# A two-layer trunk on one core: FFN up-projections by seven block products in place of eight, and the FFN split into two passes

## The chip, the core and the metric

The kernel runs on one core of one Trainium2 chip. The metric is device time in microseconds (us), the median of three runs. TensorE (PE) does the matrix products, VectorE (DVE) and GpSimd (POOL) elementwise arithmetic, ScalarE (ACT) casts and activations, and SyncE (SP) issues the DMAs, all of them in one queue, in program order.

## The reference

Two layers, sequence length 1024, model width 1024, FFN width 2816. What matters here is the second half of each layer, and the norm that stands after it:

```
x = x + gate1 * (concat(mixers(h1)) @ w_out)       # h1 = modulated RMSNorm of x
h2 = rmsnorm(x, g_ffn) * (1 + scale2) + shift2
x = x + gate2 * ((silu(h2 @ w1) * (h2 @ w3)) @ w2)  # w1, w3: 1024 x 2816; w2: 2816 x 1024
...
out = rmsnorm(x, g_final)                          # after the second layer
```

The scales, shifts and gates of a layer come from six small projections of the conditioning vector c, called the mods here.

## The kernel before, in words

x and its norms are held feature-major: eight tiles (`x[d]`, 128 features by 1024 positions), worked on in two halves of 512 positions. Every fp32 matrix product is made of three matmuls on values split into a high part (a cast on ACT, L152 for weights) and a low part (value minus high part, `sub_lo`, L160, on POOL for weights and on DVE for activations): high by high (L181), low by high (L182) and high by low (L183). A matmul has 128 by 128 weights and 512 columns. So one block of 128 outputs of an up-projection, for one half of the positions, takes 8 x 3 = 24 matmuls.

The FFN (`ffn`) goes over the 22 blocks of 128 hidden units in nine groups of two and one of four. For each group it loads blocks of w1, w3 and w2 (512 KB each, through SP), splits them, makes both up-projections of each block for both halves (`up`), applies silu (L1112), multiplies (L1113), splits the result (L1114, L160), and then adds the group's share of the down-projection to x (`down`, one accumulation of 2 x 3 matmuls per output block and half, added to x by L1121). `side()` puts pieces of the next layer's mods (L269, from 256 KB loads) between groups.

At the beginning of the FFN the norm of the second half (`norm2(1)`) isn't ready: it needs the last piece of the mixers' output projection (L1077), a sum of squares (L354, L355, and L324 on PE), a reciprocal root in twelve tiny DVE instructions (L330 to L146), its broadcast over the partitions (L339, L341 on PE, L343) and then a scaled tile (L383), its high part (L385) and its low part (L390, or L387 and L160 on POOL) for each of eight tiles. The first group makes its down-projection for the first half early, in this place: 48 matmuls that don't need that norm. At the end, the last group has four blocks, so its down-projection of the second half has 96 matmuls, and `between()`, the next norm of the first half (the next layer's, or the final one with its output stores, L1463 and L1465), is run beside them.

The instructions of each engine stand in an order that a scheduler wrote; each engine takes its own strictly in that order.

## Time and profile before

| | |
|---|---|
| median of three runs | 2955.49 us (2949.87 to 2956.98) |
| profiled execution, span from first to last instruction | 2950.3 us |
| PE busy | 2752.1 us, 93% |
| DVE, ACT, POOL busy | 57%, 38%, 27% |
| mean granted TensorE clock | 0.958 of full speed |
| FFN of layer 0, of layer 1 (about) | 808 to 1520 us, 2227 to 2928 us |

The span is that of one profiled execution; no time outside it is listed for this execution, so its span is compared with the runs' times as it stands. Matmuls are pipelined: a row's duration (0.39 us at full clock) overlaps the next one's, and the pitch from start to start is what counts.

### The profile page before, as it was taken

What the parts mean: (1) busy time and instruction counts of PE and PEld (TensorE: products, weight loads), DVE (VectorE), ACT (ScalarE), POOL (GpSimd) and SP (SyncE); (2) the same over time, 40 slices, a digit from 0 to 9 for tenths busy, and PEclk for the clock granted to TensorE, in tenths of its full rate; (3) what the DMA queues carried; (4) which work ended last, traced back from release to release, by engine and by line L of the source; (5) the groups of instructions that cost most, each with busy time, mean ns of one, the idle gap of its engine ahead of it and who ended that gap; (6) DMA issues with size and microseconds to landing.
All of it is one profiled execution on the core that took longest, in us unless ns stands there. A gap on an engine that the chain in (4) does not pass through costs nothing.

```text
span 2950.3 us, 34304 instructions
## 1 busy us (share of the span) xinstructions
PE 2752.1 (93%) x12818; PEld 2224.0 (75%) x12832; DVE 1667.1 (57%) x3456; ACT 1129.8 (38%) x2204; POOL 788.3 (27%) x412
## 2 busy tenths in 40 slices
PE   4897988999799999999999889999989999999997
PEld 4775856778678888888878667787867888888886
DVE  7579877765764444333165897787474222333215
ACT  4454777854321111111235557775342111111111
POOL 4232134441432112223231420032133222211220
PEclk9898979999999999999999988999999999999998
DMA  6102233232143222311111022112211111111101
GB/s 245 53 19 83 63 130 93 76 136 78 48 145 113 93 86 86 106 51 58 58 64 54 33 76 81 43 32 87 82 58 44 50 43 57 51 43 43 50 29 57
DMA packets 71847, 213.57 MB, mean 72 GB/s; under 512 B 9089, under 2 KB 9985, under 8 KB 71681
## 3 DMA queue, kind: packets, MB, share of 16 engines
q1 hardware_dynamic: 71680, 211.39, 21.3%
q8 instruction: 100, 1.64, 0.2%
q14 instruction: 67, 0.54, 0.1%
HBM read 184.29 MB, written 19.73 MB: 69 GB/s over the span
## 4 chain that ended last, share of the span: by engine, by line
PE 60%; DVE 8%; ACT 2%; issue 1%; POOL 0%; DMA 0%; DVEq 0%; ACTq 0%; POOLq 0%
PE tr L183 8%; PE tr L181 8%; PE tr L182 8%; PE s L181 6%; PE s L183 6%; PE s L182 6%; PE mm L181 4%; PE mm L183 4%; PE mm L182 4%; DVE jv L531 2%; PE tr L666 1%; ACT ja L528 1%; PE tr L694 1%; DVE t L383 1%; PE pv L687 1%
## 5 line engine op out<-in xcount | busy, mean ns | idle before, releaser
L160 POOL TENSOR_TENSOR wl<-raw,wh 128x1024 fp32r<-128x1024 f32 (+1 forms) x190 | 453.2, 2388 | 1262.9 <-ACT wh L152 1189.3
L152 ACT ACTIVATE wh<-raw 128x1024 fp32r<-128x1024 f32 (+2 forms) x170 | 175.1, 1033 | 752.9 <-PE mm L182 355.5
L1113 DVE TENSOR_TENSOR t<-t,tr 128x512 f32<-128x512 f32 x84 | 57.7, 687 | 581.5 <-PE tr L183 574.8
L183 PE MATMUL tr<-h,wl 128*128 128x512 f32 x928 | 368.9, 398 | 0.0
L181 PE MATMUL tr<-h,wh 128*128 128x512 f32 x928 | 368.3, 397 | 0.1
L182 PE MATMUL tr<-h,wh 128*128 128x512 f32 x928 | 367.1, 396 | 0.0
L182 PE MATMUL s<-h,wh 128*128 128x512 f32 x704 | 279.4, 398 | 5.7 <-DVE h L390 5.6
L181 PE MATMUL s<-h,wh 128*128 128x512 f32 x704 | 280.0, 398 | 5.0 <-ACT h L385 5.0
L183 PE MATMUL s<-h,wl 128*128 128x512 f32 x704 | 278.4, 395 | 0.0
L181 PEld LDWEIGHTS tr<-h,wh 128*128 128x128 f32 x928 | 175.8, 189 | 42.7 <-issue 1.2
L183 PEld LDWEIGHTS tr<-h,wl 128*128 128x128 f32 x928 | 175.5, 189 | 41.8 <-issue 1.0
L1121 DVE SCALAR_TENSOR_TENSOR x<-mm,modc,x 128x512 f32<-128x512 f32 x160 | 119.7, 748 | 153.9 <-PE mm L183 153.9
L182 PEld LDWEIGHTS tr<-h,wh 128*128 128x128 f32 x928 | 175.6, 189 | 40.4
L528 ACT ACTIVATE ja<-score,tk_t 128x384 bf16<-128x384 f32 (+2 forms) x160 | 146.0, 912 | 120.0 <-DVE tk_t L550 86.6
L642 ACT ACTIVATE P<-P,mx 128x128 f32<-128x128 f32 (+1 forms) x192 | 142.9, 745 | 62.3 <-DVE mx L639 46.7
L182 PEld LDWEIGHTS s<-h,wh 128*128 128x128 f32 x704 | 133.6, 190 | 39.0 <-DVE h L390 7.6
L181 PEld LDWEIGHTS s<-h,wh 128*128 128x128 f32 x704 | 133.5, 190 | 36.4 <-ACT h L385 5.4
L669 ACT ACTIVATE Th<-tr 128x512 fp32r<-128x512 f32 (+3 forms) x288 | 128.3, 469 | 81.2 <-PE tr L666 74.0
L183 PEld LDWEIGHTS s<-h,wl 128*128 128x128 f32 x704 | 133.3, 189 | 31.1
L160 DVE TENSOR_TENSOR Tl<-tr,Th 128x512 fp32r<-128x512 f32 (+2 forms) x232 | 131.4, 587 | 39.4 <-ACT Th L669 38.7
L666 PE MATMUL tr<-ident,P 128*128 128x128 f32 x816 | 142.1, 289 | 2.6 <-DVE y L699 1.1
L160 DVE TENSOR_TENSOR al<-t,ah 128x512 fp32r<-128x512 f32 x84 | 109.2, 1304 | 59.0 <-ACT ah L1114 46.0
(357 smaller groups left out, 6347.1 us busy)
## 6 DMA issues: line engine op xcount, KB each, us to landing
raw<-w SPq DMA_DIRECT2D x88, 512.0 KB, 3.3
mraw<-w_mod SPq DMA_DIRECT2D x48, 512.0 KB, 6.3
t<-w_mod SPq DMA_DIRECT2D x96, 256.0 KB, 4.5
raw<-ffn_w SPq DMA_DIRECT2D x44, 512.0 KB, 3.3
raw<-w_fm SPq DMA_DIRECT2D x30, 512.0 KB, 3.5
raw<-wo_abd SPq DMA_DIRECT2D x16, 384.0 KB, 3.1
x<-xT SPq DMA_DIRECT2D x16, 256.0 KB, 6.1
raw<-w_tm SPq DMA_DIRECT2D x8, 512.0 KB, 3.3
```

The lines of the kernel that those rows point to most:

```text
L152: self.nc.scalar.activation(out, in_, AF.Copy)
L160: (eng or self.nc.vector).tensor_tensor(out=out, in0=in_, in1=hi.bitcast(F32), op=ALU.subtract)
L181: self.nc.tensor.matmul(out, lh, rh, start=(i == 0), stop=False)
L182: self.nc.tensor.matmul(out, lh, rl, start=False, stop=False)
L183: self.nc.tensor.matmul(out, ll, rh, start=False, stop=(stop and i == n - 1))
L528: nc.scalar.activation(ja, score[t], AF.Sign, bias=c, scale=-1.0, accum_out=o)
L531: v.tensor_scalar(out=jv, in0=up[t] if step < 16 else score[t], scalar1=c, scalar2=0.0, op0=ALU.is_ge, op1=ALU.subtract, accum_out=o)
L642: nc.scalar.activation(P[:, 0:nk], P[:, 0:nk], AF.Exp, bias=m[:, j:j + 1], scale=-1.0, accum_out=st["rs"][:, i:i + 1])
L666: nc.tensor.transpose(p[:, i * 128:(i + 1) * 128], P[:, (kts[n] - k0) * 128:(kts[n] - k0 + 1) * 128], self.ident)
L669: nc.scalar.activation(Th[:, cs].bitcast(F32) if len(js) <= few else Th[:, cs], p[:, cs], AF.Copy)
L1113: nc.vector.tensor_tensor(out=s, in0=s, in1=p3, op=ALU.mult)
L1121: nc.vector.scalar_tensor_tensor(out=x[d][:, hs], in0=p, scalar=self.modc[l][:, 40 + d:41 + d], in1=x[d][:, hs], op0=ALU.mult, op1=ALU.add)
```

## The change

The first two blocks of the FFN are projected as before, but their down-projection isn't made early. The other 20 blocks are taken in ten pairs. Such a pair, for both halves of the positions and both halves of the width, is a 2 x 2 by 2 x 2 block product, and is made of seven block products of 4 x 3 = 12 matmuls in place of eight (Strassen's form). The sums of weight blocks that this needs (s1 to s4 of each of w1 and w3) are made on DVE for every pair, and all seven are split (cast on ACT, low part on POOL). The combinations of h2 (`combos`, t1 to t4) are made once per layer from the unsplit t tiles, which norm2 now keeps. The products' results are combined on DVE.

The hidden activations aren't split then but stored in DRAM (`aspill`), as is x (`x2spill`). In a second pass, for each half of the positions, all eight output blocks are accumulated in eight PSUM banks over all 22 blocks; w2 is loaded and split once for each half, each activation tile is loaded back and split. In the second half the first four blocks (LATE) use seven banks, then `between()` runs with the eighth bank, and then the 12 matmuls held back for that bank follow.

```diff
-            if gi == 0:
...
-                if early:
-                    side()
-                    for d in range(KD):
-                        down(d, HALVES[0])
...
+    def up_pair(self, l, fa, H, T, side):
...
+        B11, B21, B22 = H[0][0:4], H[0][4:8], H[1][4:8]
...
+        def seven(name, o, X, Y, Z):
...
+            with self.tc.high_priority(offset=PRIO):
+                W[1] = self.split_tile(a11, nc.gpsimd)
+                v.tensor_tensor(out=s1, in0=a21, in1=a22, op=ALU.add)
+                v.tensor_tensor(out=s2, in0=s1, in1=a11, op=ALU.subtract)
+                W[6] = self.split_tile(s2, nc.gpsimd)
+                W[5] = self.split_tile(s1, nc.gpsimd)
+                v.tensor_tensor(out=s3, in0=a11, in1=a21, op=ALU.subtract)
+                W[7] = self.split_tile(s3, nc.gpsimd)
+                W[2] = self.split_tile(a12, nc.gpsimd)
+                v.tensor_tensor(out=s4, in0=a12, in1=s2, op=ALU.subtract)
+                W[3] = self.split_tile(s4, nc.gpsimd)
+                W[4] = self.split_tile(a22, nc.gpsimd)
+            p1, p6, p5, p7 = [self.bank(o + i) for i in range(4)]
+            product(p1, W[1], B11, True)
+            nc.scalar.activation(X, p1, AF.Copy)
+            product(p6, W[6], T[2], True)
+            v.tensor_tensor(out=X, in0=X, in1=p6, op=ALU.add)
+            product(p5, W[5], T[1], True)
+            v.tensor_tensor(out=Y, in0=X, in1=p5, op=ALU.add)
+            product(p7, W[7], T[3], True)
+            v.tensor_tensor(out=Y, in0=Y, in1=p7, op=ALU.add)
+            product(p1, W[2], B21, False)
+            product(p5, W[3], B22, False)
+            v.tensor_tensor(out=Z, in0=X, in1=p5, op=ALU.add)
+            product(p7, W[4], T[4], False)
+            v.tensor_tensor(out=X, in0=X, in1=p7, op=ALU.add)
+            return p1
...
+        p = seven("w1", 0, X, Y, Z)
+        nc.scalar.activation(V, p, AF.Silu)
+        for t in (Y, Z, X):
+            nc.scalar.activation(t, t, AF.Silu)
+        side()
...
+        p = seven("w3", 4, X3, Y3, Z3)
+        v.tensor_tensor(out=V, in0=V, in1=p, op=ALU.mult)
...
+        for g, hs in enumerate(HALVES):
+            for d in range(KD):
+                nc.sync.dma_start(out=x[d][:, hs], in_=self.x2spill[l][d][:, hs])
+            late = LATE if g else 0
+            banks = [self.bank(d) for d in range(KD - 1 if late else KD)]
+            for f in range(NF):
+                w, y = load(f), act(f, g)
+                for d in range(len(banks)):
+                    step(banks[d], w, y, f, d)
+                if f < late:
+                    held.append((w, y))
+                if f == late - 1:
+                    between()
+                    banks.append(self.bank(KD - 1))
+                    for i, (w, y) in enumerate(held):
+                        step(banks[KD - 1], w, y, i, KD - 1)
+            for d in range(KD):
+                nc.vector.scalar_tensor_tensor(out=x[d][:, hs], in0=banks[d], scalar=self.modc[l][:, 40 + d:41 + d],
```

The first place to look at is PE's order where norm2(1) of layer 1 is made. Before, the four ones-matmuls of the sum of squares (L324) are followed by early down matmuls (their weights are `ah` and `al`), 15 of them until the first broadcast (L341), 21 more until the first matmul on the new norm:

```order
L183 MATMUL tr_19301<-ah_18963,wl_18954 128x512
L324 MATMUL pv_19176<-ones,t_19153 128x1 x4
L181 MATMUL tr_19269<-ah_19032,wh_18959 128x512
L181 MATMUL tr_19285<-ah_19032,wh_18959 128x512
L181 MATMUL tr_19301<-ah_19032,wh_18959 128x512
L182 MATMUL tr_19269<-al_19033,wh_18959 128x512
L183 MATMUL tr_19269<-ah_19032,wl_18960 128x512
```

In the changed kernel the same place reads as follows (`mh`, `ml` are the mixers' output, `h_19554` the first tile of the new norm):

```order
L181 MATMUL mm_19481<-mh_19279,wl_18669 128x512
L324 MATMUL pv_19512<-ones,t_19489 128x1 x4
L341 MATMUL mm_19538<-t_19539,ones 128x128
L341 MATMUL mm_19538<-t_19542,ones 128x128
L341 MATMUL mm_19538<-t_19545,ones 128x128
L341 MATMUL mm_19538<-t_19548,ones 128x128
L179 MATMUL s_19687<-h_19554,wh_19297 128x512
L179 MATMUL tr_19712<-h_19554,wh_19303 128x512
L179 MATMUL s_19740<-h_19554,wh_19362 128x512
L179 MATMUL tr_19765<-h_19554,wh_19368 128x512
L180 MATMUL s_19687<-h_19554,wh_19297 128x512
```

The early down matmuls are gone from between the steps of the norm, and nothing has taken their place; layer 0 reads the same.

The second place is DVE's order in a pair of layer 1, from the end of its w1 products to the sums for its w3 products (`raw_20192`, `raw_20193` are this pair's w3, `raw_20325`, `raw_20326` the next pair's w1; L1153 makes s1, L1157 s3, L1154 s2 and L1160 s4):

```order
L1171 TENSOR_TENSOR act_20059<-act_20059,tr_20094 128x512
L1174 TENSOR_TENSOR act_20058<-act_20059,tr_20093 128x512
L1176 TENSOR_TENSOR act_20059<-act_20059,tr_20094 128x512
L1153 TENSOR_TENSOR su_20196<-raw_20193 128x512
L1157 TENSOR_TENSOR su_20197<-raw_20192,raw_20193 128x512
L1153 TENSOR_TENSOR su_20329<-raw_20326 128x512
L1154 TENSOR_TENSOR su_20196<-su_20196,raw_20192 128x512
L1154 TENSOR_TENSOR su_20329<-su_20329,raw_20325 128x512
L1160 TENSOR_TENSOR su_20197<-raw_20192,su_20196 128x512
L1157 TENSOR_TENSOR su_20330<-raw_20325,raw_20326 128x512
L1160 TENSOR_TENSOR su_20330<-raw_20325,su_20329 128x512
L1167 TENSOR_TENSOR t_20189<-t_20189,s_20224 128x512
```

All sums of w3 stand behind the last addition of the w1 products (L1176), and one sum of the next pair (`su_20329`) stands ahead of s2; all sums for the next pair's w1 are made here too, a whole set of products before they are needed.

The third place is PE's order at the end of layer 1, round the final norm of the first half. Before, down matmuls stand behind L324 (33 of them until L341):

```order
L181 MATMUL mm_23351<-ah_22763,wh_22623 128x512
L182 MATMUL mm_23351<-al_22764,wh_22623 128x512
L183 MATMUL mm_23351<-ah_22763,wl_22624 128x512
L324 MATMUL pv_23258<-ones,t_23235 128x1 x4
L181 MATMUL mm_23351<-ah_22887,wh_22629 128x512
L182 MATMUL mm_23351<-al_22888,wh_22629 128x512
L183 MATMUL mm_23351<-ah_22887,wl_22630 128x512
```

In the changed kernel (`ws_23268` to `ws_23364` are the split activations of the four blocks held back, `ws_23497` the next block's):

```order
L1239 MATMUL tr_23259<-ws_23364,wl_23359 128x512
L324 MATMUL pv_23411<-ones,t_23388 128x1 x4
L341 MATMUL pv_23437<-t_23438,ones 128x128
L341 MATMUL pv_23437<-t_23441,ones 128x128
L341 MATMUL pv_23437<-t_23444,ones 128x128
L341 MATMUL pv_23437<-t_23447,ones 128x128
L1239 MATMUL pv_23476<-ws_23268,wh_23262 128x512 x2
L1239 MATMUL pv_23476<-ws_23268,wl_23263 128x512
L1239 MATMUL pv_23476<-ws_23300,wh_23294 128x512 x2
```

The 84 matmuls of the four blocks now all stand ahead of L324, and between L324 and L341 there is nothing. What comes behind the held matmuls is the block of `ws_23497`, whose load stands in SP's order behind the eight stores of the output:

```order
L1578 DMA out<-t_23467 128x512
L162 DMA raw_23874<-ffn_w 128x1024
L1578 DMA out<-t_23470 128x512
L1578 DMA out<-t_23473 128x512
L1228 DMA t_23495<-aspill_255 128x512
```

In layer 0, where the norm is the next layer's, no output is stored, but ACT's order has the norm's broadcast (L343) and eight casts (L387) and three casts of w2 ahead of the next block's activations (`ws_11865`); its last rows there are:

```order
L387 ACTIVATE h_11833<-t_11834,modc_87 128x512
L387 ACTIVATE h_11838<-t_11839,modc_87 128x512
L149 ACTIVATE wh_11859<-raw_11857 128x1024
L149 ACTIVATE wh_11894<-raw_11892 128x1024
L1093 ACTIVATE ws_11865<-t_11863 128x512
```

In before the down matmuls beside these norms used weights and activations that were split ahead of them.

## Rows read from the trace of the kernel before

**Rows 1.** The page: busy time of each engine.

```profile
PE 2752.1 (93%) x12818; PEld 2224.0 (75%) x12832; DVE 1667.1 (57%) x3456; ACT 1129.8 (38%) x2204; POOL 788.3 (27%) x412
```

**Rows 2.** Windows: PE, PEld, DVE, ACT, POOL busy us (instructions), clock, DMA share, GB/s.

```profile
1000.00:1500.00 500.00, 500.00 (x2172) 407.77 (x2171) 185.99 (x291) 86.50 (x114) 112.83 (x46) 1.00 0.23 76
1500.00:1600.00 100.00, 93.60 (x507) 80.68 (x506) 59.39 (x93) 43.85 (x78) 33.11 (x21) 0.95 0.19 65
2300.00:2900.00 600.00, 600.00 (x2602) 489.24 (x2601) 174.87 (x212) 99.48 (x131) 125.98 (x53) 1.00 0.13 44
```

**Rows 3.** Groups of instructions by line and form: busy us, mean ns, idle before.

```profile
L160 POOL TENSOR_TENSOR wl<-raw,wh 128x1024 fp32r<-128x1024 f32 x172 | 420.6, 2448 | 1152.6 <-ACT wh L152 1083.5 <-DVE t L339 31.2 <-DMA qspill<-saq 16.1
...
L160 POOL TENSOR_TENSOR wl<-raw,wh 128x512 fp32r<-128x512 f32 x2 | 2.6, 1280 | 6.3 <-ACT wh L152 6.3
...
L152 ACT ACTIVATE wh<-raw 128x1024 fp32r<-128x1024 f32 x152 | 160.3, 1058 | 719.3 <-PE mm L182 355.5 <-issue 151.7 <-PE s L182 115.6
...
L1121 DVE SCALAR_TENSOR_TENSOR x<-mm,modc,x 128x512 f32<-128x512 f32 x160 | 119.7, 748 | 153.9 <-PE mm L183 153.9
...
L1113 DVE TENSOR_TENSOR t<-t,tr 128x512 f32<-128x512 f32 x84 | 57.7, 687 | 581.5 <-PE tr L183 574.8 <-ACT t L1112 6.7
...
L1114 ACT ACTIVATE ah<-t 128x512 fp32r<-128x512 f32 x84 | 52.6, 631 | 211.3 <-DVE t L1113 210.6 <-PE tr L183 0.5
```

**Rows 4.** Timeline of PE round norm2(1), layer 1: start, us, engine, instruction, [idle before].

```profile
2213.90 0.50 PE L181 MATMUL tr<-ah,wh 128*128 128x512 f32 x1 [0.78 <-DVE s L1113]
...
2214.70 0.95 PE L324 MATMUL pv<-ones,t 128*128 128x1 f32 x8
...
2220.86 0.49 PE L341 MATMUL mm<-t,ones 128*128 128x128 f32 x2 [1.43 <-DVE t L339]
...
2221.42 0.39 PE L182 MATMUL mm<-al,wh 128*128 128x512 f32 x1
...
2228.20 0.50 PE L181 MATMUL mm<-ah,wh 128*128 128x512 f32 x1 [0.66 <-DVE x L1121]
```

**Rows 5.** Timeline of PE round norm2(0), layer 1.

```profile
2167.15 0.66 PE L181 MATMUL s<-h,wh 128*128 128x512 f32 x1 [2.67 <-ACT h L385]
...
2172.16 0.79 PE L182 MATMUL s<-h,wh 128*128 128x512 f32 x1 [3.93 <-DVE h L390]
2172.76 0.63 PE L183 MATMUL s<-h,wl 128*128 128x512 f32 x1
...
2177.74 0.39 PE L181 MATMUL s<-h,wh 128*128 128x512 f32 x1
```

**Rows 6.** Timeline of PE at the last norm, from the last down matmul on.

```profile
2928.06 0.39 PE L183 MATMUL tr<-ah,wl 128*128 128x512 f32 x1
2934.86 1.87 PE L324 MATMUL pv<-ones,t 128*128 128x1 f32 x8 [6.41 <-DVE t L355]
2939.36 2.04 PE L341 MATMUL pv<-t,ones 128*128 128x128 f32 x8 [2.64 <-DVE t L339]
```

**Rows 7.** Timeline of DVE and ACT behind that broadcast.

```profile
2942.08 5.39 DVE L1463 SCALAR_TENSOR_TENSOR t<-x,gcols,t 128x512 f32<-128x512 f32 x8 [2.27 <-ACT t L343]
...
2941.45 0.60 ACT L343 ACTIVATE t<-pv 128x512 f32<-128x512 f32 x1 [9.32 <-PE pv L341]
```

**Rows 8.** Timeline of PE: the final norm of the first half, beside down matmuls.

```profile
2911.46 0.95 PE L324 MATMUL pv<-ones,t 128*128 128x1 f32 x8
...
2920.34 1.05 PE L341 MATMUL pv<-t,ones 128*128 128x128 f32 x8
```

**Rows 9.** Timeline of DVE and of POOL in layer 0's FFN, two instructions that overlap.

```profile
933.75 2.77 DVE L160 TENSOR_TENSOR al<-t,ah 128x512 fp32r<-128x512 f32 x1
...
933.25 2.73 POOL L160 TENSOR_TENSOR wl<-raw,wh 128x1024 fp32r<-128x1024 f32 x1 [3.17 <-ACT wh L152]
```

**Rows 10.** DMA issues: engine, op xcount, KB each, median us from issue to landing.

```profile
t<-w_mod SPq DMA_DIRECT2D x96, 256.0 KB, 4.5
raw<-ffn_w SPq DMA_DIRECT2D x44, 512.0 KB, 3.3
```

More of the change, by code (lines that the diff above doesn't have):

```diff
@@ L386, in norm_chunk @@
         if k % 2:
-            nc.gpsimd.tensor_scalar(out=t, in0=t, scalar1=b[:, k:k + 1], scalar2=1.0, op0=ALU.add, op1=ALU.mult)
+            u = self.tmp() if kept else t
+            nc.gpsimd.tensor_scalar(out=u, in0=t, scalar1=b[:, k:k + 1], scalar2=1.0, op0=ALU.add, op1=ALU.mult)
+            t = u
             self.sub_lo(h[:, 1, :], t, h[:, 0, :], nc.gpsimd)
@@ new lines, in ffn, with up, act, load @@
+    def ffn(self, l, x, H, T, side, between):
+        nc = self.nc
+        ws, ys = [], [None, None]
+        def up(i, g):
+            hs = HALVES[g]
+            if g == 0:
+                ys[i] = self.slab("act")
+            p1 = self.fm_chunk(H, ws[i][0], g, self.ps("s", (128, 512), 2))
+            p3 = self.fm_chunk(H, ws[i][1], g, self.tr())
+            nc.scalar.activation(ys[i][:, hs], p1, AF.Silu)
+            nc.vector.tensor_tensor(out=ys[i][:, hs], in0=ys[i][:, hs], in1=p3, op=ALU.mult)
+        self.wlo = nc.gpsimd
+        for i in range(2):
+            ws.append((self.load_w(self.a["w1"][l, i]), self.load_w(self.a["w3"][l, i])))
+            up(i, 0)
+        yield
+        for i in range(2):
+            up(i, 1)
+            nc.sync.dma_start(out=self.aspill[l][i], in_=ys[i])
+            side()
+        for fa in range(2, NF, 2):
+            self.up_pair(l, fa, H, T, side)
+            side()
+        H.clear()
+        T.clear()
+        x[:] = [self.slab("x") for _ in range(KD)]
+        held = []
+        def act(f, g):
+            t = self.tmp()
+            nc.sync.dma_start(out=t, in_=self.aspill[l][f][:, HALVES[g]])
+            with self.tc.high_priority(offset=PRIO):
+                return self.split_tile(t, nc.vector)
+        def load(f):
+            return self.load_w(self.a["ffn_w2"][l, f * 128:(f + 1) * 128, :], base=True)
+        def step(p, w, y, f, d):
+            wh, wl = [u[:, d * 128:(d + 1) * 128] for u in w]
+            yh, yl = y[:, 0:512], y[:, 512:1024]
+            for i, (u, r) in enumerate(((wh, yh), (wh, yl), (wl, yh))):
+                nc.tensor.matmul(p, u, r, start=(f == 0 and i == 0), stop=(f == NF - 1 and i == 2))
+        for g, hs in enumerate(HALVES):
[16 more added lines that the diff above has]
+                nc.vector.scalar_tensor_tensor(out=x[d][:, hs], in0=banks[d], scalar=self.modc[l][:, 40 + d:41 + d],
+                                               in1=x[d][:, hs], op0=ALU.mult, op1=ALU.add)
+        between()
@@ L1373, in mixer, with norm2 @@
         H2 = []
-        def norm2(g, r, R=None):
-            H2.append(self.norm_half(x, self.acol[l][:, 8:16], self.modc[l][:, 24:32], g, r, self.mm, R))
+        kept = [[], []]
+        HT = {}
+        def norm2(g, r):
+            a, b = self.acol[l][:, 8:16], self.modc[l][:, 24:32]
+            R = self.stat_bcast(r, self.mm)
+            H2.append([None] * KD)
+            for k in range(4):
+                t = self.slab("t", F32, (128, 2, 512))
+                kept[g].append(t)
+                for j in range(2):
+                    H2[g][k + 4 * j] = self.norm_chunk(x, a, b, HALVES[g], R, k + 4 * j, t[:, j, :])
+            for d in range(KD):
+                nc.sync.dma_start(out=self.x2spill[l][d][:, HALVES[g]], in_=x[d][:, HALVES[g]])
+            if g:
+                HT.update(self.combos(*kept, b))
         rr = []
```

145 lines of the change are left out of this document (66 added, 79 removed).

## The prediction

> **What bounds the kernel now.** I read the page first, then the windows, then the groups by line, then the timeline wherever PE was not busy. The page shows PE busy for 93% of the span, DVE for 57%, ACT 38%, POOL 27% [rows 1]. An average says little, so the windows come next: in both FFNs PE is busy for every microsecond, at full granted clock, while DVE works some 30 to 37 us of 100, POOL 21 to 23 and ACT 17 [rows 2]. So in this stage only PE's matmuls set the time, and the pitch is 500 / 2172 = 0.2302 us and 600 / 2602 = 0.2306 us from one start to the next; I use 0.2304. A matmul less is 0.23 us less, as long as PE stays fed. The timeline shows why it is fed so well: at norm2(1) PE runs early down matmuls between the steps of the norm and idles only 0.78, 1.43 and 0.66 us [rows 4]; at the final norm of the first half it goes straight through, 8.9 us from L324 to L341 [rows 8]. Where nothing stands between, as at the last norm, PE waits 6.41 and 2.64 us [rows 6].
>
> **What is removed.** A pair of hidden blocks took 2 x 2 x 2 x 24 = 192 up matmuls and takes 2 x 7 x 12 = 168. Ten pairs, two layers: 20 x 24 = 480 matmuls, 480 x 0.2304 = 110.6 us. The down matmuls keep their number (22 x 8 x 2 x 3 in both forms). Everything else is what is lost of these 110.6 us.
>
> **A: norm2(1) without cover.** The order shows L324, L341 and the first matmuls on the new norm with nothing between, in both layers. So PE waits through the chain. Its parts: from the last projection to L324 about 1.6 us (2214.70, less the 2213.1 at which PE fell idle ahead of 2213.90, with what it did between left out); from L324 to L341 4.50 us undisturbed [rows 6], of which 0.95 is L324 itself: 3.55; then norm2(0), which has no cover already now, shows what follows L341: 2.67 us idle until the first high part, 3.93 until the first low part [rows 5]. Together 11.75, less the 2.87 idle there now [rows 4]: 8.9 us a layer. Behind it comes the clock: after those two idles matmuls took 0.63 us in place of 0.39 until 2177.7 [rows 5]; some 17 of them at 0.43 us a pitch are 17 x 0.2 = 3.4 us. 12.3 a layer, 24.6 for both. `combos` puts 16 combinations and 8 low parts on DVE behind the norm, about 24 x 0.7 = 17 us by L1113's 687 ns [rows 3], against 96 + 12 matmuls, 25 us, of PE work that starts after the norm's first tile and shares that time with its remaining tiles: I add 2 us a layer. **A = +29**, rounded up. Its bounds: 12, if the low part comes at once and the clock holds; 50, if POOL holds DVE up in norm and combinations.
>
> **B: the change from w1 to w3 in a pair.** Let T be the end of the last w1 product. All sums of w3 stand behind its addition (the order of DVE), and one sum of the next pair is ahead of s2. The addition ends at T + 0.2 + 0.75 (an eviction, 748 ns), and four sums of 0.69 take DVE to T + 3.7; I take L1113's 687 ns for a sum [rows 3], since before has none. Its cast, half a tile wide, is 0.63 on ACT and its low part 1.28 on POOL [rows 3]: T + 4.4 and T + 5.7. PE meanwhile has the first product, which needs no sum: 12 x 0.23 = 2.76, and about 0.3 for its own low part: T + 3.06. So it waits 1.3 us for the cast, then does six high-part matmuls as three casts arrive (0.63 each against 0.46), and is past the low part at about T + 6.1: 2.0 us idle in a pair, 40 in all 20. The other direction, w3 to the next w1, costs nothing, since those sums are ready. Single idles of 1.4 us left the clock up: behind 1.43 us the matmuls still show 0.39 [rows 4]. In layer 0 the mods' instructions stand in some of these places too: +2. **B = +42**, with 10 (the casts run ahead) and 90 (4.5 us a pair) as ends.
>
> **C and D: the second pass.** Its beginning needs w2 and activations that are loaded and split while the last products run: +2 (0 to 12). In its steady course a block of one half has 24 matmuls, 5.53 us. Against that stand 512 KB of w2, landing in 3.3 us [rows 10], a cast of 1.06 and a low part of 2.45 us [rows 3], a chain of 6.8 us, of which two buffers make 3.4 us a block; POOL alone needs 2.45, ACT 1.06 + 0.63, DVE one low part. The evictions of L1121, 160 for each of two sets of banks [rows 3], fall from 320 to 32. All hidden under PE: 0 (0 to 10).
>
> **E: the norm beside four blocks.** The 84 matmuls stand ahead of L324, 19.4 us, which more than covers the eight evictions and the sums of squares; but between L324 and L341 nothing is left: 3.55 us idle. Then PE has L341 and 12 held matmuls, 0.8 + 2.8 = 3.6 us. In layer 1 the next activations are loaded behind the eight stores: from L341 to L1463 2.72 us, its eight instructions 5.39 [rows 6, 7], then a 256 KB load (4.5 us as for the mods, 3.3 as for twice the size of weights [rows 10]; I take 4.0) and a cast, 0.63: 12.7 after L341, so 9.1 idle. In layer 0 the broadcast's end (2.1 us after L341 [rows 6, 7]), eight casts paced by DVE at about 1 us, three of w2 at 1.06 and one of 0.63 come to 13.9: 10.3 idle. With 3.4 for the clock each time, as in A: 3.55 + 9.1 + 3.4 = 16, and 17. **E = +33** (20 to 48); now it costs nothing [rows 8].
>
> **G: the end of layer 0.** The next layer's norm of the first half is ready far earlier than now. Of the 6.4 us idle there now [rows 2] I give back 3: **-3**. The last norm's tail is unchanged: eight evictions and the sums as at 2928.06 to 2934.86 [rows 6].
>
> **The sum.** -110.6 + 29 + 42 + 2 + 0 + 33 - 3 = -7.6 us on the span of 2950.3. That span lies 5.2 under the median of the runs and inside their spread, so I apply the difference to the median: 2947.9, rounded 2948.
>
> **A rule weighed.** A low part on DVE took 2.77 us and ended 0.54 us after the POOL instruction that had started ahead of it [rows 9], where an operation of that size beside no such work is 0.69 [rows 3]. So DVE can lose 2 us to one low part on POOL. In B it shouldn't: by the order POOL is free from about T + 0.7 until s2 is done. The Trainium skill, "SBUF — State Buffer", section "SBUF: two separate sides", says that DVE, with two inputs in SBUF, and a GpSimd instruction that reads SBUF lock each other out for a whole instruction. By that rule the two rows are as they should be, and a sum for the next set that starts just ahead of the first low part would push it by an estimated 0.69 us a pair, 14 us in all, which would make the sum +6 in place of -7.6.
>
> **The rivals.** *The waits are hidden.* If ACT and DVE come to the w3 sums early, B is 10, A 12 and E 20: -110.6 + 12 + 10 + 20 - 3 = -72, 2884 us. Against it speaks the strict order. *The clock falls in every pair* (the other side). B's idle of 2.0 us lies between the 1.43 that left the clock up [rows 4] and the 2.67 and 3.93 behind which it was down [rows 5]. If one sum or low part is held up by 0.7 us, a third of what rows 9 show, and the clock's fall costs 3.4 each time: 20 x 4.1 = 82, 3030 us. It decides when a pair loses more than (110.6 - 29 - 2 - 33 + 3) / 20 = 2.5 us in all, its wait and its slow matmuls together. *w2 bounds the down pass.* If the two buffers didn't overlap, a block would take 6.8 us and not 5.53: 1.27 x 88 = +112, 3060 us. The windows would show PE idle all through the second pass; POOL's 2.45 and DMA's 3.3 speak against it.
>
> **How the numbers follow.** My forecast has a chance of 0.50, hidden waits 0.25, the clock in every pair 0.20, w2 0.05. The likeliest case alone is 2925 to 2968. Both signs hold much of the chance, so the range is wide: 2870 takes in nearly all of the hidden case, 3015 the lower third of the clock case and leaves out the rest and w2. About 0.3%, 9 us, is what a measurement of this kernel can tell from no change. Half of the likeliest case and all of the hidden one, less a little, are faster by more: 0.46. Within it: two fifths of the likeliest, 0.20. Slower: the rest of the likeliest and the last two cases, 0.34.
>
> **What would show it.** A: PE idle of some 10 us at norm2(1), 0.63 us matmuls behind it. B: in each pair an idle of about 1.3 us ahead of the second w3 product, by the cast of s2, then some tenths; if that idle is 0 B is wrong, if it is 2.5 or the clock of the windows in the up pass is under 1.00, the rival is right. E: two idles, 3.5 us ahead of L341 and 9 to 10 behind the held matmuls. D: windows of the second pass at PE 100%. The forecast falls if the matmuls themselves keep another pitch than 0.2304.

## The result and the profile after

| | before | after |
|---|---|---|
| median in the same comparison | 2952.68 us | 2979.71 us (2977.92 to 2981.84) |
| ratio | | 1.0095, interval 1.008 to 1.011 |
| profiled execution, span | 2950.3 us | 2977.4 us |
| mean granted TensorE clock | 0.958 | 0.941 |
| moved by DMA | 213.57 MB | 299.64 MB |

The changed kernel is 0.95% slower. The forecast was a gain of 7.6 us; the two spans show a loss of 27.1. The time lies inside the range, on the other side of no change, and 35 us are to be found.

The page of after, busy time of each engine, answers to [rows 1]:

```profile
PE 2713.4 (91%) x12352; PEld 2150.8 (72%) x12352; DVE 1850.7 (62%) x3578; ACT 1297.9 (44%) x2520; POOL 1122.6 (38%) x672
```

PE has 480 matmuls less (PEld's counts with those of [rows 1]; 14 of before's records on PE are missing), and its share fell: it waits more. The windows of after (columns as in [rows 2]): the pairs, then the second pass, both of layer 1.

```profile
2400.00:2500.00 100.00, 98.30 (x416) 77.04 (x416) 40.44 (x51) 24.89 (x43) 41.62 (x30) 1.00 0.27 95
2700.00:2800.00 100.00, 100.00 (x428) 80.40 (x427) 38.80 (x20) 36.30 (x43) 63.28 (x26) 1.00 0.52 177
```

In 100 us of a steady pass before, PE did 434 [rows 2: 500 us, 2172]. Now the pairs do 416, with 2 us idle and the clock at 1.00, and the second pass does 428 although PE is never idle there. Of these, 426 start inside the window (a count has those that reach over its edges too), 0.2343 us from start to start. That pitch belongs to no wait.

The steady pair, PE's timeline in layer 1 (a row can stand for several matmuls, the count at its end):

```profile
2292.55 5.76 PE L1139 MATMUL tr<-h,ws 128*128 128x512 f32 x24
2298.15 3.29 PE L1139 MATMUL mm<-h,ws 128*128 128x512 f32 x12
2302.22 0.73 PE L1139 MATMUL s<-h,ws 128*128 128x512 f32 x2 [0.78 <-ACT ws L1093]
...
2343.03 0.73 PE L1139 MATMUL s<-h,ws 128*128 128x512 f32 x2 [0.78 <-ACT ws L1093]
```

From one wait for the cast of s2 to the next it is 40.81 us, for 168 matmuls: 168 x 0.2304 = 38.71, so 2.1 us are lost in a pair. The 24 matmuls of the first row take 2298.15 - 2292.55 = 5.60, a pitch of 0.2333. At that pitch 168 take 39.2, so of the 2.1 us about 1.6 are waits and 0.5 is pitch.

The same place on DVE and ACT, 40.8 us on, shows the chain that part B of the prediction derived: last addition, four sums with one of the next pair ahead of s2, three casts.

```profile
2339.16 0.69 DVE L1176 TENSOR_TENSOR act<-act,tr 128x512 f32<-128x512 f32 x1 [2.11 <-PE tr L1139]
2339.77 0.68 DVE L1153 TENSOR_TENSOR su<-raw 128x512 f32<-128x512 f32 x1
2340.37 0.68 DVE L1157 TENSOR_TENSOR su<-raw,raw 128x512 f32<-128x512 f32 x1
2340.97 0.69 DVE L1153 TENSOR_TENSOR su<-raw 128x512 f32<-128x512 f32 x1
2341.57 1.29 DVE L1154 TENSOR_TENSOR su<-su,raw 128x512 f32<-128x512 f32 x2
2342.35 1.67 ACT L1093 ACTIVATE ws<-su 128x512 fp32r<-128x512 f32 x3 [1.83 <-DVE su L1154]
```

The first pair of a layer is another matter. PE's timeline in layer 0, from the start of that pair's w1 products to that of its w3 products:

```profile
829.25 0.63 PE L1139 MATMUL mm<-h,ws 128*128 128x512 f32 x2
831.88 3.85 PE L1139 MATMUL mm<-h,ws 128*128 128x512 f32 x10 [1.99 <-POOL ws L157]
...
839.86 0.50 PE L1139 MATMUL s<-h,ws 128*128 128x512 f32 x1 [1.61 <-ACT h L1109]
845.90 1.22 PE L1139 MATMUL s<-h,ws 128*128 128x512 f32 x2 [5.54 <-DVE h L157]
...
858.97 7.42 PE L1139 MATMUL tr<-h,ws 128*128 128x512 f32 x24 [2.12 <-DVE act L1169]
869.76 0.73 PE L1139 MATMUL mm<-h,ws 128*128 128x512 f32 x2 [3.37 <-ACT ws L1093]
```

The second product of the pair (the tile `s`) waits 5.54 us for a low part of t2 (`h`, L157 on DVE). On DVE that is the seventh of the eight low parts that it makes for the combinations, 29.8 us after the first combination began (814.25), and it runs beside one on POOL:

```profile
844.09 1.76 DVE L157 TENSOR_TENSOR h<-t,h 128x512 fp32r<-128x512 f32 x1
...
843.58 1.72 POOL L157 TENSOR_TENSOR h<-t,h 128x512 fp32r<-128x512 f32 x1
```

The same instruction took 0.68 us at 824.69, where POOL was idle. The groups of after by line and form say why (L1116, L1118, L1120 and L1123 are the four combinations, L157 with `h` the low parts of two of them, both layers together):

```profile
L157 DVE TENSOR_TENSOR h<-t,h 128x512 fp32r<-128x512 f32 x16 | 21.6, 1356 | 0.0
L1120 DVE SCALAR_TENSOR_TENSOR t<-t,db 128x512 f32<-128x512 f32 x8 | 12.1, 1512 | 0.0
L1116 DVE TENSOR_TENSOR t<-t,t 128x512 f32<-128x512 f32 x8 | 12.0, 1502 | 0.0
L1118 DVE SCALAR_TENSOR_TENSOR t<-t,modc,t 128x512 f32<-128x512 f32 x8 | 10.6, 1322 | 0.2
L1123 DVE SCALAR_TENSOR_TENSOR t<-t,modc,t 128x512 f32<-128x512 f32 x8 | 9.0, 1123 | 0.0
```

They take (21.6 + 12.1 + 12.0 + 10.6 + 9.0) / 2 = 32.7 us a layer, not the 17 that the prediction allowed.

norm2(1), layer 1, where [rows 4] showed early down matmuls between the steps:

```profile
2233.22 1.05 PE L324 MATMUL pv<-ones,t 128*128 128x1 f32 x8 [2.29 <-DVE t L355]
2236.82 2.08 PE L341 MATMUL mm<-t,ones 128*128 128x128 f32 x8 [2.55 <-DVE t L339]
2241.12 0.79 PE L179 MATMUL s<-h,wh 128*128 128x512 f32 x1 [2.23 <-ACT h L387]
...
2243.02 0.79 PE L180 MATMUL s<-h,wh 128*128 128x512 f32 x1
```

And PE's timeline at the final norm of the first half, where it went straight through in [rows 8]:

```profile
2830.71 0.95 PE L324 MATMUL pv<-ones,t 128*128 128x1 f32 x8
2834.30 2.04 PE L341 MATMUL pv<-t,ones 128*128 128x128 f32 x8 [2.65 <-DVE t L339]
2837.03 1.22 PE L1239 MATMUL pv<-ws,wh 128*128 128x512 f32 x2 [0.69 <-ACT t L343]
...
2853.01 0.79 PE L1239 MATMUL mm<-ws,wh 128*128 128x512 f32 x1 [11.63 <-ACT ws L1093]
```

Behind it on DVE, the eight instructions that answer to the first of [rows 7]:

```profile
2837.01 9.60 DVE L1576 SCALAR_TENSOR_TENSOR t<-x,gcols,t 128x512 f32<-128x512 f32 x8 [2.27 <-ACT t L343]
```

PE idles 2.65, 0.69 and 11.63 us. Layer 0 has 2.64, 0.69 and 8.91 in the same place.

**Where the 27.1 us are.** Sizes of losses are time beyond the count of matmuls at 0.2304 us, the prediction's own measure, net of what before lost in the same place.

| part | forecast | measured, both layers |
|---|---|---|
| 480 matmuls removed | -110.6 | -110.6 |
| A, norm2(1), without the combinations | 25 | 13 |
| B and the combinations (2 a layer): all pairs | 46 | 77 |
| E, the norm beside four blocks | 33 | 36 |
| C, D and all else in the FFN (by difference) | 2 | 16 |
| G and the stages outside the FFN | -3 | -5 |
| sum | -7.6 | +27 |

A: the idles 2.29 + 2.55 + 2.23 and some 2.4 us for the clock (4.96 us from the first start at 2241.12 to the twelfth at 2246.08, in place of 11 x 0.2304; most of these matmuls take 0.63 us), less 2.87: 6.6 a layer. Pairs: 431.5 us in layer 0 and 420.0 in layer 1, less 387.1 each: 44.4 and 32.9; ten steady pairs would lose 21 of each, so the first pairs lose 23 and 12 beyond that. Of the 77 us, 3360 x (0.2333 - 0.2304) = 10 are pitch and not waits. E: 17.2 and 18.5, of which the idles are 12.2 and 15.0. The FFN as a whole, from the last projection to its last matmul, grew by 22.9 and 8.9 us.

### The profile page after: what moved, and what is told of

The parts are those of the page before. It is cut to its first block, busy times and chain, and to the rows that moved or that the text cites. A ratio compares the mean times of both kernels' runs of the same rounds, so it can differ in the third digit from the quotient of the medians.

```text
span 2977.4 us, 35101 instructions
## 1 busy us (share of the span) xinstructions
PE 2713.4 (91%) x12352; PEld 2150.8 (72%) x12352; DVE 1850.7 (62%) x3578; ACT 1297.9 (44%) x2520; POOL 1122.6 (38%) x672
## 2 busy tenths in 40 slices
DMA packets 106417, 299.64 MB, mean 101 GB/s; under 512 B 12928, under 2 KB 13824, under 8 KB 106240
## 4 chain that ended last, share of the span: by engine, by line
PE 53%; DVE 10%; ACT 3%; issue 2%; DMA 2%; POOL 1%; DVEq 0%; SPq 0%; ACTq 0%; POOLq 0%
PE tr L1139 11%; PE mm L1139 5%; PE tr L1239 5%; PE s L1139 4%; PE mm L1239 4%; PE s L1239 4%; PE pv L1139 4%; DVE jv L535 2%; PE pv L1239 2%; PE mm L181 2%; PE mm L179 2%; PE mm L180 2%; PE tr L670 1%; DVE t L385 1%; DMA raw<-ffn_w 1%
## 5 line engine op out<-in xcount | busy, mean ns | idle before, releaser
L157 POOL TENSOR_TENSOR wl<-raw,wh 128x1024 fp32r<-128x1024 f32 (+1 forms) x154 | 366.6, 2384 | 527.4 <-ACT wh L149 345.3
L1139 PE MATMUL tr<-h,ws 128*128 128x512 f32 x1440 | 359.0, 400 | 2.1 <-DVE act L1169 2.1
L1139 PEld LDWEIGHTS tr<-h,ws 128*128 128x128 f32 x1440 | 273.2, 191 | 72.4 <-ACT ws L1093 4.3
L157 POOL TENSOR_TENSOR ws<-raw,ws 128x512 fp32r<-128x512 f32 x120 | 171.9, 1438 | 356.9 <-ACT ws L1093 356.7
L157 DVE TENSOR_TENSOR ws<-t,ws 128x512 fp32r<-128x512 f32 x88 | 147.6, 1692 | 233.4 <-ACT ws L1093 233.4
L1139 PE MATMUL mm<-h,ws 128*128 128x512 f32 x960 | 253.5, 403 | 10.4 <-POOL ws L157 5.9
L157 POOL TENSOR_TENSOR ws<-su,ws 128x512 fp32r<-128x512 f32 x160 | 228.3, 1446 | 66.9 <-ACT ws L1093 66.8
L1139 PEld LDWEIGHTS mm<-h,ws 128*128 128x128 f32 x960 | 181.2, 191 | 63.0 <-POOL ws L157 16.6
L1239 PE MATMUL tr<-ws,wh 128*128 128x512 f32 x528 | 169.9, 400 | 0.0
L1139 PE MATMUL s<-h,ws 128*128 128x512 f32 x480 | 131.8, 409 | 25.0 <-ACT ws L1093 12.8
L157 DVE TENSOR_TENSOR Tl<-tr,Th 128x512 fp32r<-128x512 f32 (+2 forms) x232 | 131.7, 587 | 34.4 <-ACT Th L673 33.6
L535 DVE TENSOR_SCALAR_CACHE_REDUCE jv<-up,tk_t 128x896 bf16<-128x896 bf16 (+3 forms) x128 | 120.8, 944 | 4.5 <-POOL up L513 1.9
```

The source lines that it names most:

```text
L157: (eng or self.nc.vector).tensor_tensor(out=out, in0=in_, in1=hi.bitcast(F32), op=ALU.subtract)
L535: v.tensor_scalar(out=jv, in0=up[t] if step < 16 else score[t], scalar1=c, scalar2=0.0, op0=ALU.is_ge, op1=ALU.subtract, accum_out=o)
L1139: nc.tensor.matmul(p, u, r, start=first and k == 0 and i == 0, stop=k == 3 and i == 2, skip_group_check=not first)
L1239: nc.tensor.matmul(p, u, r, start=(f == 0 and i == 0), stop=(f == NF - 1 and i == 2))
```

## The experiments

Each run has the kernel before beside it on the same chip; "against before" and "against after" are differences of medians, where after stands 27.0 above its own before.

**1. The sums of w3 made early.** The two tiles of w3 are taken and loaded ahead of their pair's activation tiles, and the sums lie in four half-size tiles with seven buffers in place of two whole ones with three.

```diff
+        early = [self.slab("raw") for _ in range(2)]
+        for r, f in zip(early, (fa, fa + 1)):
+            nc.sync.dma_start(out=r, in_=self.a["w3"][l, f])
...
-            ra, rb = [self.slab("raw") if o else self.raw(None) for _ in range(2)]
+            ra, rb = early if o else [self.raw(None) for _ in range(2)]
...
-            su, sv = [self.rp.tile([128, 1024], F32, tag="su", bufs=NSUM, name=self.nm("su")) for _ in range(2)]
-            s1, s2, s3, s4 = su[:, 0:512], su[:, 512:1024], sv[:, 0:512], sv[:, 512:1024]
+            s1, s2, s3, s4 = [self.rp.tile([128, 512], F32, tag="su", bufs=7, name=self.nm("su")) for _ in range(4)]
```

> Edit to the changed kernel: the two w3 tiles of a pair are allocated and loaded ahead of its activation tiles, and the four weight sums lie in four half-size tiles (seven buffers) in place of two whole ones (three buffers). By the order, DVE then makes all sums of w3 one set of products ahead, and no product waits for one. Theory (the pair's wait is the chain addition, four sums, cast, low part behind the last w1 product): the pitch of a steady pair falls from 40.82 us by about 2 us to 38.8, in 17 to 20 pairs, and the time by 34 to 42 us, to about 2941. Rival (the matmuls of a pair are slowed by the work on DVE and POOL beside them, or the clock): the pitch stays at 40.5 or more and the time falls by less than 8 us.

Measured: 2947.63 us, ratio 0.9999 (0.9985 to 1.0013): 2.3 under before, 29 under after. PE's timeline in layer 1 has no idle in a steady pair any more:

```profile
2308.73 5.76 PE L1139 MATMUL tr<-h,ws 128*128 128x512 f32 x24
2314.33 2.96 PE L1139 MATMUL mm<-h,ws 128*128 128x512 f32 x12
...
2325.53 2.96 PE L1139 MATMUL s<-h,ws 128*128 128x512 f32 x12
```

The pairs lose 29.8 and 20.4 in place of 44.4 and 32.9: 27 us, where 20 pairs of 1.6 us of waits would be 32; 34 to 42 were expected. The waits went and the pitch is still 5.60 / 24 = 0.2333, so late sums were the wait in the pairs, as B said, and not slower matmuls or the clock. The edit changes the place of the loads and the buffers of the sums at once; which of the two let the sums come early, no run takes apart.

**2. Two blocks of the second pass ahead of the norm.** The blocks 4 and 5 are loaded and split before `between()`.

```diff
+            ahead = {}
...
-                w, y = load(f), act(f, g)
+                w, y = ahead.pop(f) if f in ahead else (load(f), act(f, g))
...
                 if f == late - 1:
+                    for e in range(late, late + 2):
+                        ahead[e] = (load(e), act(e, g))
                     between()
```

> Edit to the changed kernel: in the second half of the down pass the loads and splits of the two blocks that follow the four with a held-back bank stand ahead of the norm in the program, not behind it. By the order PE then has 36 of their matmuls between the sum of squares and the broadcast. Theory (the two idles there, 2.6 us ahead of the broadcast and 8.9 and 11.6 us ahead of the next block, and the low clock behind them are what this place costs): 12 to 15 us less in each layer, 24 to 30 in all, about 2953. Rival (the stores of the output and ACT's casts only hold up the block after those two in the same way): the idle moves behind them, and 10 us or less come back.

Measured: 2968.01 us, ratio 1.0066 (1.0044 to 1.0089): 9 under after. PE's timeline at the final norm:

```profile
2841.55 1.05 PE L341 MATMUL pv<-t,ones 128*128 128x128 f32 x8
2857.15 0.80 PE L1239 MATMUL mm<-ws,wh 128*128 128x512 f32 x1 [7.98 <-ACT ws L1093]
```

SP's timeline there (the stores of the output, and the load for block 6):

```profile
2844.05 8.65 SPq L1581 DMA_DIRECT2D out<-t  x7
2853.18 0.33 SPq L1228 DMA_DIRECT2D t<-aspill  x1
```

The wait ahead of L341 is gone. The one behind the held matmuls is not: it has moved to block 6, whose activations are issued behind seven stores. In layer 0 it is 16.31 us, more than the three idles there before (2.64, 0.69 and 8.91), so nothing is gained in that layer. There no store stands in the way; PE goes on when ACT has cast block 6's activations, directly behind the norm's casts and one of weights:

```profile
1432.73 0.80 PE L1239 MATMUL mm<-ws,wh 128*128 128x512 f32 x1 [16.31 <-ACT ws L1093]
...
1430.49 0.72 ACT L387 ACTIVATE h<-t,modc 128x512 fp32r<-128x512 f32 x1 [1.99 <-DVE t L385]
...
1432.07 0.61 ACT L1093 ACTIVATE ws<-t 128x512 fp32r<-128x512 f32 x1
```

Their load, too, was issued only at 1427.17. Cover of two blocks moves the wait; what makes it is what stands in front of the next load and cast. In the code the activations and the norm's outputs take their buffers from the same `tmp`; that this is what holds the loads is read from the code, and no run changed it.

**3. No combinations.** The products read tiles of h2 as they are; the combinations and their splits are left out.

```diff
-                HT.update(self.combos(*kept, b))
+                HT.update({1: H2[1][0:4], 2: H2[1][4:8], 3: H2[0][4:8], 4: H2[0][0:4]})
```

> Edit to the changed kernel: the combinations of the norm's tiles (t1 to t4 and their splits) are left out, and tiles of the norm itself stand in their place, so the FFN's result is another one. All products keep their number and size. Theory (in each layer the first pairs wait for the combinations, which stand on DVE behind the norm and are held up by POOL): the first two pairs of layer 0 lose 23 us less and the first of layer 1 12 us less, the time falls by 30 to 36 us, to about 2946. Rival (the first pairs wait for the weights or for the rest of the norm): 10 us or less come back.

Measured: 2951.19 us, ratio 1.0005 (0.9986 to 1.0024): 26 under after. The pairs lose 26.6 and 24.6: 18 and 8 less. So the combinations cost some 26 us, where A had 4 for them; of the 35 us that the first pairs lose beyond the steady loss, some 9 stay without them. In layer 0 PE waits nowhere in the first pair but at s2, so the waits of after at 858.97 and 869.76, which stand behind the mods and behind w3's load, came from the combinations as well.

**4. The activations of the second pass in the big buffers.** They are split into a tile of the pool that holds w2's split tiles, in place of the FFN's own pool.

```diff
-                return self.split_tile(t, nc.vector)
+                y = self.slab("ys", F32R)
+                nc.scalar.activation(y[:, 0:512], t, AF.Copy)
+                self.sub_lo(y[:, 512:1024], t, y[:, 0:512], nc.vector)
+                return y
```

> Edit to the changed kernel: in the down pass the split activations (what the matmuls stream) lie in the pool of the norm's and x's tiles and not in the pool of the split up weights. Theory (a matmul with one operand in the pool of the up weights has a longer pitch: 0.2324 us in the up and 0.2272 in the down pass of the kernel before, 0.2336 in the down pass of the changed one): the pitch of the down pass falls to about 0.2275, 2112 x 0.006 = 12 us, about 2967. Rival (the pitch follows the order of banks and weights from one matmul to the next): no change of the pitch, within 3 us of 2980.

Measured: 2946.79 us, ratio 0.9995 (0.998 to 1.001): 30 under after. The activations get other buffers with it, and layer 0's six short waits behind the norm (5.0 us in all, five of them for a low part on DVE) are gone; at the final norm 11.63 became 3.71, beside the norm of layer 0 8.91 became 9.52. But something else came with it. The same window as in after, where PE did 428:

```profile
2700.00:2800.00 100.00, 100.00 (x443) 82.81 (x442) 55.85 (x33) 33.81 (x45) 46.86 (x19) 1.00 0.41 140
```

443, of which 441 start inside, a pitch of 0.2267 in place of 0.2343, with nothing changed in the matmuls but where one operand lies. The up pass, which this edit doesn't touch, kept 5.60 us for 24. In after w2's tiles start at 128 modulo 256 bytes of a partition and the activations at 32; with this edit both start at 128.

**5. The FFN's pool moved by 32 bytes.** A small constant ahead of it changes nothing but its address (its tiles start at 64 modulo 256).

```diff
+        pad = self.const.tile([128, 8], F32, name="pad")
+        nc.vector.memset(pad, 0.0)
```

> Edit to the changed kernel: a tile of 32 bytes more among the constants. It moves the pool of the split weights and activations from byte 180512 of each partition (32 past a multiple of 64) to 180544 (a multiple of 64); nothing else changes. In the run with the activations in the slabs the pitch of the down pass was 0.2260 us in place of 0.2336. Theory A (the start of the streamed operand within 64 bytes sets the pitch): the down pass falls to 0.2260 to 0.2280 here too, 12 to 16 us less, about 2965. Theory B (what counts is that the operands of a matmul lie in two pools far apart in SBUF, as for the up matmuls of the kernel before, 0.2324 us with a pool that begins on a multiple of 256): 0.2320 to 0.2340, within 4 us of the changed kernel.

Measured: 2960.99 us, ratio 1.004 (1.0022 to 1.0058): 17 under after. The timeline of PE in the pairs:

```profile
2308.77 5.66 PE L1141 MATMUL tr<-h,ws 128*128 128x512 f32 x24
2314.27 2.91 PE L1141 MATMUL mm<-h,ws 128*128 128x512 f32 x12
```

(2314.27 - 2308.77) / 24 = 0.2292, from 0.2333. In the second pass, where the activations lie in the moved pool and not the weights, it is 0.2333, from 0.2343 (428 starts from 2700 to 2800 us). Neither theory had it so. Every engine keeps its order, but for the one instruction that fills the constant: an address alone moves the pitch.

**6 and 7. Edits 1, 2 and 4 together, and these with four plain blocks.** The latter projects blocks 2 and 3 as the first two are, so that the pairs begin one pair later, with 24 matmuls more in each layer.

```diff
-        for fa in range(2, NF, 2):
+        for i in range(2, 4):
+            ws.append((self.load_w(self.a["w1"][l, i]), self.load_w(self.a["w3"][l, i])))
+            ys.append(None)
+            up(i, 0)
+            up(i, 1)
+            nc.sync.dma_start(out=self.aspill[l][i], in_=ys[i])
+        for fa in range(4, NF, 2):
```

> The edits of e1_sums_early, e2_two_blocks_ahead and e4_activations_in_slabs together, the reference's whole computation. Alone they took 30, 10 and 31 us off the changed kernel's FFNs, 27 of e1's in the pairs and 31 of e4's in the down pass. Theory (the losses lie in places of their own, and the next block's wait in e2 came from the six small buffers that activations and the norm's outputs share): the pairs lose 30 and 20 us as in e1, the down passes 12 or less each, about 2912 to 2922, 1.0 to 1.3% faster than the kernel before. Rival (what is taken off at the pairs comes back as contention in the down pass or the other way round): 2935 or more.

> The three edits of e6 and one more: the first four blocks of each FFN are projected in the plain way, and nine pairs follow. This gives back 2 x 24 matmuls, 11 us, and puts 88 matmuls more, some 22 us, between the second norm and the first pair. Theory (the first pairs only wait for combinations that are late): the 26 us that e3 gave without the combinations come back, 15 us less than e6. Rival (the combinations cost what they do because they hold up DVE and POOL wherever they stand): the first pairs wait no less, 11 us more than e6.

Measured: 2903.69 us, ratio 0.9842 (0.9824 to 0.9859), and 2897.04 us, 0.9813 (0.9794 to 0.9831). The three edits gave 29, 9 and 30 alone and give 75 together, a little more than their sum of 68 and than was expected. The plain blocks add 6.6 where 15 were expected, and the two intervals just overlap; the profiled executions differ by 15.7 (spans 2902.2 and 2886.5), but that of the seventh lies 9 us under its own median, so the medians stand.

**8. Four plain blocks alone.**

> The changed kernel with only this edit: the first four blocks in the plain way, nine pairs. Theory (the combinations are late): the loss of the first pairs, 23 us in layer 0 and 12 in layer 1, goes, for 11 us of matmuls that come back: 20 to 25 us less, about 2957. Rival (they cost their work wherever they stand): 5 to 12 us more, about 2988.

Measured: 2964.76 us, ratio 1.0047 (1.0032 to 1.0062): 13 under after. Nine pairs take 367.8 and 368.8 us: 1512 x 0.2304 = 348.4, so 2.2 us lost in each, the steady loss and no more. What the first pair lost is gone, though DVE has the same combinations to make. The time fell by less than the 20 to 25 us expected, since more came back than the 48 matmuls (11 us): ahead of the pairs, the 288 matmuls of the plain blocks lose 8.4 and 6.4 us beyond 0.2304 each, where the 96 of after lose 3.0 in each layer. A part of these 9 us, in layer 0:

```profile
832.29 0.80 PE L181 MATMUL s<-h,wl 128*128 128x512 f32 x1 [2.27 <-POOL wl L157]
```

That low part of weights starts on POOL at 829.44, directly behind low parts of combinations. So the larger part of the combinations' cost was that they were late; that they are many is left beside the plain blocks, on POOL.

**9. All of the combinations' low parts on DVE.** POOL had two of four.

```diff
-            split(1, t1, nc.gpsimd)
+            split(1, t1, nc.vector)
...
-            split(3, t3, nc.gpsimd)
+            split(3, t3, nc.vector)
```

> Edit to the changed kernel: the low parts of the combinations t1 and t3, on POOL so far, are made on DVE like those of t2 and t4. It gives DVE 8 more instructions a layer and takes 8 of 1.6 us from POOL. In the changed kernel DVE's combinations beside POOL took 1.3 to 1.5 us each, where such an operation alone is 0.69. Theory (the combinations are late because POOL's instructions hold DVE's up): DVE's instructions there fall to 0.7 to 1.0 us and the first pairs lose 5 to 15 us less over both layers. Rival (DVE simply has too much to do there): 8 x 0.7 = 6 us more on DVE in each layer, the first pairs lose the same or up to 12 us more.

Measured: 2973.28 us, ratio 1.0081 (1.0065 to 1.0096): 5 under after, and the two ratios' intervals overlap, so the time alone doesn't decide. In the profiled executions the pairs lose 38.6 and 29.8, 9 less. The group of DVE's low parts, which answers to the first of the groups of after:

```profile
L157 DVE TENSOR_TENSOR h<-t,h 128x512 fp32r<-128x512 f32 x32 | 26.6, 866 | 0.0
```

Twice as many low parts cost DVE 26.6 us in place of 21.6, 866 ns each in place of 1356, and L1116 fell from 1502 to 1087 ns. DVE has 16 instructions more and is done earlier, because POOL, which still splits weights then, has fewer. The Trainium skill, "SBUF — State Buffer", section "SBUF: two separate sides", says that such a DVE instruction and a GpSimd one that reads SBUF keep each other out for a whole instruction; the trace agrees: with an instruction on POOL beside it such a DVE instruction took 1.76 us, without one 0.68, and with fewer on POOL the mean falls as above.

**10 and 11. The pool moved until both start alike, in the kernel after and in the kernel before.** 96 bytes in after (all start at 128 modulo 256 then). In before the FFN's pool starts at 0 modulo 256 and is moved by 128, with the same result.

```diff
+        pad = self.const.tile([128, 24], F32, name="pad")
```
```diff
+        pad = self.const.tile([128, 32], F32, name="pad")
```

> Edit to the changed kernel: as e5_pool_moved_32_bytes, but 96 bytes, so that the pool of split weights and activations begins on byte 180608, 128 past a multiple of 256, as the pool of the norm's tiles does. Pitches so far: 0.2313 us (up) and 0.2336 (down) with the pool 32 past; 0.2256 and 0.232 with it 64 past; 0.2260 with both operands in the other pool; 0.2324 in the kernel before, where the two pools' starts differ by 128 in 256. Theory (the two operands' places within 256 bytes, one against the other, set the pitch): 0.226 in both passes, 20 to 25 us less than the changed kernel, 2955 to 2960. Rival (the distance of the pools does): the down pass stays at 0.232 or more.

> The kernel before with one edit: 128 bytes more among the constants, so that its pool of split weights begins on byte 195968 in place of 195840, 128 past a multiple of 256 like the pool of the norm's tiles. Its 4224 up matmuls ran at 0.2324 us and its 2112 down matmuls, both operands in the other pool, at 0.2272. Theory (places within 256 bytes): the up matmuls fall to 0.2260 to 0.2275, 20 to 27 us less, 2925 to 2932. Rival (distance of the pools): the same within 6 us.

Measured: 2945.71 us, ratio 0.9981 (0.9967 to 0.9995), 32 under after; and 2919.06 us, 0.9902 (0.9883 to 0.992), 32 under before. In the moved after, PE's timeline in the pairs:

```profile
2298.60 5.60 PE L1141 MATMUL tr<-h,ws 128*128 128x512 f32 x24
2304.04 2.88 PE L1141 MATMUL mm<-h,ws 128*128 128x512 f32 x12
```

5.44 / 24 = 0.2267. Both fell further than was expected. Of the pitches listed in the first expectation, those with the pool 64 past are 0.2292 and 0.2333 from start to start, and 0.2260 is 0.2267. In the moved before, the window that had 434 matmuls:

```profile
2400.00:2500.00 100.00, 100.00 (x443) 82.81 (x442) 34.54 (x43) 15.51 (x20) 21.55 (x9) 1.00 0.14 48
```

Again 441 start inside: 0.2267. So the places of the operands cost either kernel 1.1%, and they don't explain the result: with both moved the change is still slower, 2945.71 / 2919.06 = 1.009.

**12. All of it: edits 1, 2 and 4, four plain blocks, the pool moved by 96 bytes.**

> The kernel of e7_three_edits_four_plain with the pool moved by 96 bytes as in e10. Theory (places within 256 bytes): its 3408 up matmuls of the pairs and plain blocks run at 0.226 in place of 0.229 to 0.231, 8 to 15 us less, 2882 to 2890, 2.2 to 2.5% faster than the kernel before. Rival (distance of the pools): 2892 to 2902 as e7.

Measured: 2872.15 us, ratio 0.9734 (0.9719 to 0.9749), 79 under before and 106 under after; against the moved kernel before, 2872.15 / 2919.06 = 0.984. So the form itself is worth 1.6% here, 47 us, once most of its waits are covered; its 432 matmuls less come to 99.5 us at 0.2304. What is left on PE's timeline in the second pass:

```profile
1348.32 0.73 PE L1253 MATMUL s<-ys,wh 128*128 128x512 f32 x2 [3.23 <-DVE x L1275]
1386.88 0.80 PE L1253 MATMUL mm<-ys,wh 128*128 128x512 f32 x1 [8.27 <-ACT ys L1242]
...
2761.12 0.79 PE L1253 MATMUL mm<-ys,wh 128*128 128x512 f32 x1 [3.46 <-ACT ys L1242]
```

## Why the prediction was wrong, step by step

**Its frame held.** PE's matmuls and waits set the time; 480 matmuls less are worth 110.6 us at 0.2304, and waits and a longer pitch took more than that back. Of the rivals none came: the waits are not hidden, the clock is 1.00 in the window of the steady pairs, and PE is never idle in the window of the second pass, so w2 does not bound it.

**The step that failed: "I add 2 us a layer" for the combinations, in A.** Measured: 23 and 12 us beyond the steady pairs' loss, and 26 us in all in experiment 3, for 4: 22 of the 31 us by which the pairs are off, and the largest single term. Two things were wrong in it. The size: 24 instructions at 0.7 us are 17, but they took 32.7, since POOL splits weights and its own share of the combinations at the same time. The rule weighed in the prediction speaks of just this, and was weighed for the pairs alone; there the sums stayed at 0.68. Experiment 9 shows the effect; what it took away, 9 us, is the smaller part. The comparison: 17 us of DVE were held against 25 us of PE's work as if they were due at its end. `combos` goes through the four tiles one by one, t1 to t4 for each, so the last tile of t2, which the second product needs, comes near the end of all 24; PE wanted it 12 matmuls into the first pair. Experiment 8, which only lets PE come later, takes the whole loss of the first pair away; of 35 us, 9 come back beside the plain blocks. In layer 0 the delay also reached the mods and this pair's w3; experiment 3 shows that, not by which buffer.

**D, "0", failed as well, for a reason that no step considered.** In the window of the second pass everything of DVE, ACT, POOL and DMA was hidden, as said; only layer 0 had six short waits behind the norm, 5.0 us. But the 2112 matmuls ran at 0.2343. I had taken one pitch, 0.2304, as a mean over both kinds of matmuls; apart, in before's timeline in layer 1, 182 starts of up matmuls and 53 of down matmuls give 0.2324 and 0.2274:

```profile
2330.49 0.39 PE L181 MATMUL s<-h,wh 128*128 128x512 f32 x1
...
2372.78 0.40 PE L183 MATMUL tr<-h,wl 128*128 128x512 f32 x1
2373.01 0.40 PE L181 MATMUL mm<-ah,wh 128*128 128x512 f32 x1
...
2385.06 0.40 PE L183 MATMUL tr<-ah,wl 128*128 128x512 f32 x1
```

Against before's own down matmuls that is 2112 x (0.2343 - 0.2274) = 15 us. In the table, which measures by the mean of both kinds, it is 2112 x (0.2343 - 0.2304) = 8 of the 16; layer 0's 5.0 and 1.8 at the two beginnings of the second pass, for which C had 2, leave about 1 open. The last sentence of the prediction's text named this way to fall without giving it a price.

**B held in its size, 42 for 2.1 us a pair,** and its mechanism is the one that experiment 1 removes. In it, the wait is 1.6 us rather than 2.0, and the other 0.5 is pitch, so that the size agrees partly by luck. "T + 4.4" for the cast was right to some tenths: the last addition begins at 2339.16, which the prediction puts at T + 0.2, and PE goes on at 2343.03, T + 4.1.

**A's chain was too dear.** The idle of 3.93 us for the first low part, taken over from norm2(0), didn't come: the low part at 2243.02 follows with no wait. The forecast's 12.3 a layer was 6.6.

**E held,** 36 for 33. The parts were not all of the right size: the eight instructions on DVE took 9.60, not 5.39, and the wait behind them 11.63, not 9.1; layer 0's was 8.91, not 10.3. **G held,** -4.2 for -3: from the last down matmul of layer 0 to the next layer's first product on its `h` it was 36.3 us and is 32.1.

So in the forecast's own sum: 31 us too little for the pairs, 14 too little for the second pass, 3 for E, and 12 too much for A: 36, of which 2 came back outside the FFN. To rounding, that is the difference of 35.

## What to carry to other kernels

Work that is new in a pipeline is priced by when its first needed piece is due, in the order in which it is made, and not by its total beside the time of the work that covers it. When a change takes instructions out of the bounding engine, count what each of its waits now finds in front of it on the other queues: here most of the saved 110 us were spent on sums, combinations and loads that stood behind something else, and putting them earlier, or their first use later, won about half of it back with all the combinations still made. And a pitch is measured for each kind of instruction by itself, with the places of its operands: a mean over two kinds foretells neither.

## What the runs showed of the hardware

The pitch of a 128x512 matmul with both operands in SBUF, at granted clock 1.00 and without idle, hung on where its two operands start within 256 bytes of a partition. With the FFN's pool 96 bytes short of the other it was 0.2333 us where the weights lie in that pool (up pass) and 0.2343 where the streamed activations do (second pass); with 64 bytes, 0.2292 and 0.2333 (experiment 5); with 128, 0.2324 (before's up matmuls); with both alike, 0.2267 to 0.2274 (before's down matmuls, whose operands lie in one pool, and experiments 4 and 10 to 12). So the distance alone does not set it: which operand lies where, or another difference between the two passes, counts too. Placing both alike was worth 32 us, 1.1%, of either kernel. The runs show that the address alone does it (experiments 5, 10 and 11); why is open, as no run took apart the matmul's own reads and other engines' accesses.
